# A two-level triangular inverse on TensorE: matrices 0 to 3 and 4 to 7 alternate between two quarters of the array

## The chip, the cores and the metric

The kernel runs on one core of one Trainium2 chip. The metric is the device time of one execution in microseconds (us), the median over runs. The clock that the throttle granted TensorE is listed with each run, as a share of full speed; it was 0.997 in the profiled execution.

## What is computed

The reference is one step of a decoder layer in float32: a gated DeltaNet branch (32 value heads of 128 x 128 state, 16 query and key heads) and a sparse attention branch, on 256 prompt tokens and on 8 samples of 8 tokens, 320 tokens in all; model width 2048. The change touches the delta rule's triangular solve, cut here to what matters (a block has 64 tokens in the reference):

```python
def gated_delta_rule(q, k, v, g, beta, s0):
    # chunked (WY form): S_t = e^{g_t} S_{t-1} + k_t beta_t (v_t - e^{g_t} S_{t-1}^T k_t)^T
    ...
    kb = k * beta[..., None]
    a_strict = jnp.where(strict, jnp.einsum('bhnid,bhnjd->bhnij', kb, k) * decay, 0.0)
    rhs = jnp.concatenate([v * beta[..., None], kb * jnp.exp(G)[..., None]], axis=-1)
    sol = lax.linalg.triangular_solve(a_strict, rhs, left_side=True, lower=True, unit_diagonal=True)
    u_intra, w_state = sol[..., :DV], sol[..., DV:]
    ...
    def chunk_step(s, xs):
        u_c, w_c, qk_c, qd_c, kt_c, gt_c = xs
        u = u_c - jnp.einsum('bhck,bhkv->bhcv', w_c, s)
        o = jnp.einsum('bhck,bhkv->bhcv', qd_c, s) + jnp.einsum('bhij,bhjv->bhiv', qk_c, u)
        s = s * gt_c[..., None, None] + jnp.einsum('bhck,bhcv->bhkv', kt_c, u)
        return s, o
    s, o = lax.scan(chunk_step, s0, xs)
    ...
```

The kernel takes blocks of 128 prompt tokens, and inverts the unit triangular matrices instead of solving with them.

## The kernel before

**The main stream.** `stream()` goes over all weights in half-blocks of 128 x 8 x 128 numbers. For exactness each is split into two parts, `whi` (ScalarE's rounded copy of `raw`) and `wlo` (VectorE's remainder), and so are the activations (`xh`, `xl`). A unit of the stream is 24 matmuls of 128 x 128 x 320 into a main PSUM bank (`pm`): eight pairs `xh,whi` and `xl,whi`, then eight `xh,wlo`. SP loads `raw` several half-blocks ahead (three tiles of two halves).

**The side work.** All else that needs TensorE stands between main matmuls. After the sixth pair of a unit and at its end, so after every 12 main matmuls, `side_round()` steps each of a list of generators once; a step emits its instructions and yields. The program's order is thus fixed when it is built, by a planner (`Clock`) with modelled costs: a generator may yield a due time, and `need(self.ps_side, n)` lets it go on only when n of the side PSUM banks (`ps`, six, 128 x 512 numbers each) are free and, by the model, idle. `psum()` takes the bank that is idle earliest. Each engine runs its own instructions in that order and waits on semaphores where data or buffers come from another. TensorE runs in order, so a side matmul that waits holds the main stream behind it.

**The inverse.** The generator `inverse(g, G)` runs for eight groups g, each of two heads with twelve unit triangular 128 x 128 matrices: eight of the prompt (m = 0 to 7) and four of the samples. The four diagonal 32 x 32 blocks of each matrix go to 48 partitions and are inverted on GpSimd in 31 steps. The result in both orientations goes to DRAM (`d_x[0]`, `d_x[1]`) and comes back spread over partitions, as do the off-diagonal blocks (`d_o`). The tiles: `blk` holds BO (off-diagonal 64 x 64 blocks), BD (off-diagonal 32 x 32 blocks) and Q1; `Xt`, shown as X in the profile, holds XB (inverse, 64-row quarter) and Q2; `XT` is the result, twelve transposed inverses. Then four stages on TensorE build the prompt matrices' off-diagonal parts, each stage one bank and one step of the generator, with at least 12 main matmuls between two stages:

1. Q1 = BD·XB, 32 x 32, in rows 0:32 and 64:96 of the array alternately: 16 matmuls.
2. 32 x 32, the off-diagonal blocks of XT at both 64-row halves, and the lower left block of XB: 24 matmuls.
3. 64 x 64, Q2 = BO·XB, all in rows 0:64 with results in partitions 64:128: eight matmuls.
4. 64 x 64, XT's upper right quarter = −Q2·XT, all in rows 64:128 with results in partitions 0:64: eight matmuls.

ScalarE evicts each result (`self.act`). Behind stage 4 `G["T"] = 4` lets the chains of the group's two heads start (`prompt_chain`, `sample_chain`), which use XT, vt, kq, ktok and w. The tiles of the inverse and XT have one buffer each, so one group's inverse follows the other's.

All loads and stores named here are issued on SP's queue, in program order, among the loads of `raw`.

Of the kernel before, what the change touches and what calls it, by code (L numbers as in the profile page):

```python
# [11 lines left out]
AF = mybir.ActivationFunctionType  # L12
# [189 lines left out]
class Kernel:  # L202
# [1668 lines left out]
    def inverse(self, g, G):  # L1871
        nc = self.nc
        BT = G["BT"]
        d_b, d_x, d_o = self.d_b[g % 2], self.d_x[g % 2], self.d_o[g % 2]
        yield self.ready(BT)
        for k in range(4):
            nc.sync.dma_start(d_b[k].rearrange("m j i -> j m i"), BT[32 * k:32 * k + 32, :, 32 * k:32 * k + 32])
        nc.sync.dma_start(d_o[:, :, 0:64], BT[0:64, 0:8, 64:128])
        for o in (0, 64):
            nc.sync.dma_start(d_o[o // 2:o // 2 + 32, :, 64:96], BT[o:o + 32, 0:8, o + 32:o + 64])  # L1880
        self.BT.put(BT)
        yield
        yield from self.need(self.inv)
        tiles = blk, Xt = self.inv.get()
        yield self.idle(blk, Xt)
        nc.sync.dma_start(blk[0:48], d_b.rearrange("k m j i -> (k m) (j i)"))
        nc.gpsimd.memset(Xt[0:48], 0.0)
        nc.gpsimd.memset(Xt[0:48, 0:1024:33], 1.0)
        yield
        X = Xt[0:48].rearrange("p (i c) -> p i c", c=32)  # L1890
        B = blk[0:48].rearrange("p (j i) -> p j i", i=32)
        for j in range(31):
            n, m = 31 - j, j + 1
            t = self.tmp[:, 0:n * m].rearrange("p (i c) -> p i c", c=m)
            bv = B[:, j, j + 1:32].rearrange("p (i o) -> p i o", o=1).to_broadcast([48, n, m])
            xv = X[:, j:j + 1, 0:m].to_broadcast([48, n, m])
            self.tt(t, bv, xv, OP.mult, eng=nc.gpsimd)
            self.tt(X[:, j + 1:32, 0:m], X[:, j + 1:32, 0:m], t, OP.subtract, eng=nc.gpsimd)
            if j % 4 == 4 - 1:
                yield self.clock.last - 3.6  # L1900
        nc.gpsimd.tensor_copy(blk[0:48].rearrange("p (c i) -> p c i", i=32), X.rearrange("p i c -> p c i"))
        yield
        while not self.XT.free:
            yield
        XT = G["XT"] = self.XT.get()
        XB = Xt[:, 0:512].rearrange("p (m c) -> p m c", c=64)
        Q2 = Xt[:, 512:1024].rearrange("p (m c) -> p m c", c=64)
        BO = blk[:, 0:512].rearrange("p (m c) -> p m c", c=64)
        BD = blk[:, 512:768].rearrange("p (m c) -> p m c", c=32)
        Q1 = blk[:, 768:1024].rearrange("p (m c) -> p m c", c=32)  # L1910
        nc.sync.dma_start(d_x[0].rearrange("k m i c -> (k m) (i c)"), Xt[0:48])
        nc.sync.dma_start(d_x[1].rearrange("k m i c -> (k m) (i c)"), blk[0:48])
        yield max(self.clock.last, self.idle(XT))
        nc.gpsimd.memset(XB[0:32, :, 32:64], 0.0)
        nc.sync.dma_start(BO[0:64], d_o[:, :, 0:64])
        for o in (0, 64):
            nc.sync.dma_start(BD[o:o + 32], d_o[o // 2:o // 2 + 32, :, 64:96])
        for k in range(4):
            s = slice(32 * k, 32 * k + 32)
            nc.sync.dma_start(XT[s, :, s], d_x[1][k].rearrange("m i c -> i m c"))  # L1920
            if k < 3:
                o = 32 * (k % 2)
                nc.sync.dma_start(XB[s, :, o:o + 32], d_x[0][k, 0:8].rearrange("m i c -> i m c"))
        yield
        yield from self.need(self.ps_side)
        p = self.psum()
        pv = p[:, 0:256].rearrange("p (m c) -> p m c", m=8)
        for m in range(8):
            for o in (0, 64):
                self.mm(pv[o + 32:o + 64, m, :], BD[o:o + 32, m, :], XB[o:o + 32, m, 0:32], skip=True)  # L1930
        for o in (32, 96):
            self.act(Q1[o:o + 32], pv[o:o + 32])
        self.ps_side.put(p)
        yield
        yield from self.need(self.ps_side)
        p = self.psum()
        pv = p.rearrange("p (e m c) -> p e m c", e=2, m=8)
        for m in range(8):
            for o in (0, 64):
                self.mm(pv[o:o + 32, 0, m, :], Q1[o + 32:o + 64, m, :], XT[o + 32:o + 64, m, o + 32:o + 64], skip=True)  # L1940
            self.mm(pv[32:64, 1, m, :], XT[32:64, m, 32:64], Q1[32:64, m, :], skip=True)
        for o in (0, 64):
            self.act(XT[o:o + 32, 0:8, o + 32:o + 64], pv[o:o + 32, 0], AF.Copy, scale=-1.0)
        self.act(XB[32:64, :, 0:32], pv[32:64, 1], AF.Copy, scale=-1.0)
        self.ps_side.put(p)
        yield
        yield from self.need(self.ps_side)
        p = self.psum()
        pv = p.rearrange("p (m c) -> p m c", m=8)
        for m in range(8):  # L1950
            self.mm(pv[64:128, m, :], BO[0:64, m, :], XB[0:64, m, 0:64], skip=True)
        self.act(Q2[64:128], pv[64:128])
        self.ps_side.put(p)
        yield
        yield from self.need(self.ps_side)
        p = self.psum()
        pv = p.rearrange("p (m c) -> p m c", m=8)
        for m in range(8):
            self.mm(pv[0:64, m, :], Q2[64:128, m, :], XT[64:128, m, 64:128], skip=True)
        self.act(XT[0:64, 0:8, 64:128], pv[0:64], AF.Copy, scale=-1.0)  # L1960
        self.ps_side.put(p)
        self.inv.put(tiles)
        G["T"] = 4
        self.inverses += 1
# [454 lines left out]
```

## Time and profile before

| | us |
|---|---|
| median of three runs | 2175.32 |
| runs | 2173.44 to 2176.6 |
| profiled execution | 2176.31 |
| its span in the profile | 2174.6 |
| TensorE busy | 2144.6 |
| VectorE busy | 1395.1 |
| ScalarE busy | 995.3 |
| GpSimd busy | 462.2 |

The profiled execution has 1.71 us outside the span. A row of the page's groups gives line, engine, operation, output and inputs by the program's names, the shape and the count, then busy time, the mean in ns and the idle time before. All instructions pass through one helper, so all rows have line L61, and one goes by tile names. An fp32 matmul has two records in the profile: `ps<-XT,X 64*64 64x64 f32 x16` are eight matmuls on a 64 x 64 part of the array with 64 columns each. PE is TensorE's matmuls, PEld its weight loads, DVE VectorE, ACT ScalarE, POOL GpSimd, SPq SP's issue of DMAs. A timeline row begins with its start and duration; consecutive instructions of a group are one row, with their count at the end.

### The profile page before, as it was taken

The page shows a single profiled execution, that of the slowest core. Times are in us where ns is not written, and L with a number is a line of the kernel's source. Part 1 is how long each engine was busy: PE and PEld are TensorE (multiplying, and loading weights), DVE is VectorE, ACT ScalarE, POOL GpSimd, SP SyncE. Part 2 cuts the span into 40 slices and gives each one's busy share as a digit, 9 for nine tenths or more (in the row PEclk, how much of TensorE's full clock was granted, in tenths as well). Part 3 has the DMA queues.
Part 4 walks back from the last instruction along what each step waited for, and adds up shares of the span by engine and source line. Part 5 has one row for each costly group of instructions (what it writes and reads, how often), then busy time and mean ns, then how long its engine had stood idle before and what let it go on. Part 6 is the DMA issues. An engine that isn't in the chain of part 4 may idle for free.

```text
span 2174.6 us, 43708 instructions
## 1 busy us (share of the span) xinstructions
PE 2144.6 (99%) x17071; PEld 2045.5 (94%) x17071; DVE 1395.1 (64%) x2823; ACT 995.3 (46%) x2217; POOL 462.2 (21%) x627
## 2 busy tenths in 40 slices
PE   7999999999999999999999999999999999999997
PEld 6889988999999999899999999999999999999997
DVE  4665545789754577877877777877746545455443
ACT  3225465333343455465555555555545434333343
POOL 1001000000001018353636362626260000000000
PEclk9999999999999999999999999999999999999999
DMA  9995656975688666776768686867786867555562
GB/s 328 356 290 152 172 152 185 273 225 154 180 244 246 192 180 174 203 209 184 206 191 221 176 215 180 217 176 210 185 238 192 261 188 214 166 149 155 156 183 87
DMA packets 715087, 438.38 MB, mean 202 GB/s; under 512 B 69088, under 2 KB 700224, under 8 KB 712576
## 3 DMA queue, kind: packets, MB, share of 16 engines
q1 hardware_dynamic: 710784, 412.92, 67.3%
q0 software_dynamic: 3616, 21.02, 2.9%
q8 instruction: 134, 2.20, 0.4%
q10 hardware_dynamic: 480, 1.65, 0.3%
q14 instruction: 73, 0.60, 0.1%
HBM read 386.29 MB, written 48.94 MB: 200 GB/s over the span
## 4 chain that ended last, share of the span: by engine, by line
PE 68%; issue 23%; DVE 5%; ACT 2%; DMA 2%; SPq 0%; DVEq 0%; POOL 0%; POOLq 0%; ACTq 0%
PE pm L61 52%; PE ps L61 16%; DVE S L61 2%; DMA raw<-in_w_ada_dram 1%; DVE ps L61 1%; ACT ot L61 1%; DVE wlo L61 1%; DVE w L61 0%; ACT whi L61 0%; ACT vt L61 0%; DMA c<-in_c_sample_dram 0%; SPq L61 0%; DVE vt L61 0%; DVE sc L61 0%; DVE sga L61 0%
## 5 line engine op out<-in xcount | busy, mean ns | idle before, releaser
L61 PE MATMUL pm<-xh,whi 128*128 128x320 f32 x3284 | 1004.1, 319 | 2.0 <-ACT whi L61 1.7
L61 PE MATMUL pm<-xl,whi 128*128 128x320 f32 x3284 | 971.6, 309 | 0.3 <-DVE xl L61 0.3
L61 DVE TENSOR_TENSOR wlo<-raw,whi 128x1024 fp32r<-128x1024 f32 x474 | 593.1, 1259 | 291.0 <-ACT whi L61 275.6
L61 PEld LDWEIGHTS pm<-xh,whi 128*128 128x128 f32 x3284 | 616.8, 188 | 39.6 <-issue 31.2
L61 PEld LDWEIGHTS pm<-xl,whi 128*128 128x128 f32 x3284 | 617.5, 188 | 1.6 <-DVE xl L61 0.8
L61 ACT ACTIVATE whi<-raw 128x1024 fp32r<-128x1024 f32 x474 | 498.9, 1059 | 169.1 <-PE pm L61 151.0
L61 PE MATMUL pm<-xh,wlo 128*128 128x320 f32 x3284 | 553.3, 309 | 0.0
L61 PEld LDWEIGHTS pm<-xh,wlo 128*128 128x128 f32 x3284 | 499.5, 188 | 0.0
L61 POOL TENSOR_TENSOR X<-X,tmpx 48x31 f32<-48x31 f32 (+15 forms) x248 | 180.6, 728 | 19.5
L61 POOL TENSOR_TENSOR tmpx<-blk,X 48x31 f32<-48x31 f32 (+15 forms) x248 | 160.4, 647 | 55.1 <-DMA blk<-d_b 23.4
L61 PE MATMUL pm<-y1h,whi 128*128 128x320 f32 x512 | 151.8, 310 | 1.9 <-ACT y1h L61 1.9
L61 PE MATMUL pm<-y1l,whi 128*128 128x320 f32 x512 | 151.9, 310 | 0.1
L61 DVE SCALAR_TENSOR_TENSOR ps<-xp,cs,ps 128x344 f32<-128x344 f32 x192 | 111.5, 581 | 6.8
L61 POOL TENSOR_TENSOR sc<-sc,mh 128x6 f32<-128x6 f32 (+1 forms) x24 | 44.7, 1864 | 324.9 <-DVE ct L61 165.4
L61 POOL TENSOR_TENSOR rfin<-rfin,mh 128x3 f32<-128x3 f32 x1 | 0.8, 848 | 489.4 <-DVE rfin L61 489.4
L61 PEld LDWEIGHTS pm<-y1h,whi 128*128 128x128 f32 x512 | 96.6, 189 | 2.2 <-ACT y1h L61 2.2
L61 PEld LDWEIGHTS pm<-y1l,whi 128*128 128x128 f32 x512 | 96.6, 189 | 0.7 <-DVE y1l L61 0.6
L61 PE MATMUL pm<-y1h,wlo 128*128 128x320 f32 x512 | 86.4, 311 | 0.0
L61 PEld LDWEIGHTS pm<-y1h,wlo 128*128 128x128 f32 x512 | 78.5, 190 | 0.0
L61 DVE SCALAR_TENSOR_TENSOR S<-S,gtr,ps 128x128 f32<-128x128 f32 x256 | 67.4, 341 | 0.1
L61 ACT ACTIVATE ot<-ot,sc 128x128 f32<-128x128 f32 x96 | 29.9, 390 | 74.2 <-DVE sc L61 74.2
L61 ACT ACTIVATE xp<-pm 128x256 f32<-128x256 f32 (+1 forms) x128 | 32.0, 304 | 67.6 <-PE pm L61 67.6
(368 smaller groups left out, 2329.7 us busy)
## 6 DMA issues: line engine op xcount, KB each, us to landing
raw<-in_w_in_dram SPq DMA_DIRECT2D x336, 512.0 KB
raw<-in_w_pa_dram SPq DMA_DIRECT2D x64, 512.0 KB
rawx<-in_w_ada_dram SPq DMA_DIRECT2D x18, 1024.0 KB
a<-in_w_ada_dram SPq DMA_DIRECT2D x16, 1024.0 KB
S<-in_state_gdn_dram SPq DMA_DIRECT2D x32, 512.0 KB
out_dram<-S SPq DMA_DIRECT2D x32, 512.0 KB
raw<-in_w_pb_dram SPq DMA_DIRECT2D x32, 512.0 KB
raw<-in_w_out_dram SPq DMA_DIRECT2D x32, 512.0 KB
```

The costliest lines, as they stand in the source:

```text
L61: made = fn(*args, **kw)
```

## The change

All of it is in `inverse`. Matrices 0 to 3 stay in the quarters of the array where all eight were; matrices 4 to 7 of stages 3 and 4 go to another quarter, and the matmuls alternate between the two. For that BO of matrices 4 to 7 is loaded to partitions 64:128, and a new piece of the tile Xt, XE, holds the inverse's blocks that these matrices need on the other partitions: four more loads from `d_x`, two more memsets on GpSimd. In stage 2, half of the XB products go to the other partitions, and four more products give XE's second block in a second bank; there are three evictions to XB and XE (ahead of XT's two) where there was one. Stage 3 fills one bank's 256 columns on all 128 partitions and has one eviction; stage 4 fills two banks and has two.

```diff
-        Q2 = Xt[:, 512:1024].rearrange("p (m c) -> p m c", c=64)
+        Q2 = Xt[:, 512:768].rearrange("p (m c) -> p m c", c=64)
+        XE = Xt[:, 768:1024].rearrange("p (m c) -> p m c", c=64)
...
         nc.gpsimd.memset(XB[0:32, :, 32:64], 0.0)
-        nc.sync.dma_start(BO[0:64], d_o[:, :, 0:64])
+        nc.gpsimd.memset(XE[32:64, :, 0:32], 0.0)
+        nc.gpsimd.memset(XE[64:96, :, 32:64], 0.0)
+        for e in range(2):
+            nc.sync.dma_start(BO[64 * e:64 * e + 64, 0:4], d_o[:, 4 * e:4 * e + 4, 0:64])
...
+            o, t = 32 * (k % 2), 32 * ((k + 2) % 4)
+            nc.sync.dma_start(XE[t:t + 32, :, o:o + 32], d_x[k // 2][k, 4:8].rearrange("m i c -> i m c"))
...
-        yield from self.need(self.ps_side)
-        p = self.psum()
+        yield from self.need(self.ps_side, 2)
+        p, q = self.psum(), self.psum()
         pv = p.rearrange("p (e m c) -> p e m c", e=2, m=8)
+        qv = q[:, 0:128].rearrange("p (m c) -> p m c", m=4)
         for m in range(8):
             for o in (0, 64):
                 self.mm(pv[o:o + 32, 0, m, :], Q1[o + 32:o + 64, m, :], XT[o + 32:o + 64, m, o + 32:o + 64], skip=True)
-            self.mm(pv[32:64, 1, m, :], XT[32:64, m, 32:64], Q1[32:64, m, :], skip=True)
+            o = 64 * (m // 4)
+            self.mm(pv[o + 32:o + 64, 1, m, :], XT[32:64, m, 32:64], Q1[32:64, m, :], skip=True)
+            if m > 3:
+                self.mm(qv[0:32, m - 4, :], Q1[96:128, m, :], XT[96:128, m, 96:128], skip=True)
+        self.act(XB[32:64, 0:4, 0:32], pv[32:64, 1, 0:4], AF.Copy, scale=-1.0)
+        self.act(XE[96:128, :, 0:32], pv[96:128, 1, 4:8], AF.Copy, scale=-1.0)
+        self.act(XE[0:32, :, 32:64], qv[0:32], AF.Copy, scale=-1.0)
         for o in (0, 64):
             self.act(XT[o:o + 32, 0:8, o + 32:o + 64], pv[o:o + 32, 0], AF.Copy, scale=-1.0)
-        self.act(XB[32:64, :, 0:32], pv[32:64, 1], AF.Copy, scale=-1.0)
...
-        pv = p.rearrange("p (m c) -> p m c", m=8)
-        for m in range(8):
+        pv = p[:, 0:256].rearrange("p (m c) -> p m c", m=4)
+        for m in range(4):
             self.mm(pv[64:128, m, :], BO[0:64, m, :], XB[0:64, m, 0:64], skip=True)
-        self.act(Q2[64:128], pv[64:128])
+            self.mm(pv[0:64, m, :], BO[64:128, m, :], XE[64:128, m, :], skip=True)
+        self.act(Q2, pv)
...
-        yield from self.need(self.ps_side)
-        p = self.psum()
-        pv = p.rearrange("p (m c) -> p m c", m=8)
-        for m in range(8):
-            self.mm(pv[0:64, m, :], Q2[64:128, m, :], XT[64:128, m, 64:128], skip=True)
-        self.act(XT[0:64, 0:8, 64:128], pv[0:64], AF.Copy, scale=-1.0)
+        yield from self.need(self.ps_side, 2)
+        banks = [self.psum() for _ in range(2)]
+        for m in range(4):
+            self.mm(banks[0][0:64, 64 * m:64 * m + 64], Q2[64:128, m, :], XT[64:128, m, 64:128], skip=True)
+            self.mm(banks[1][0:64, 64 * m:64 * m + 64], Q2[0:64, m, :], XE[0:64, m, :], skip=True)
+        for e, p in enumerate(banks):
+            self.act(XT[0:64, 4 * e:4 * e + 4, 64:128], p[0:64, 0:256].rearrange("p (m c) -> p m c", m=4), AF.Copy, scale=-1.0)
```

The planner's model prices the instructions as they are written, so the order moves too. In the first and seventh inverse the stages stand where they stood; in the second and eighth all four stages come one round later; in the third to sixth stages 1 and 2 stand where they stood and stages 3 and 4 come one round later. In those, the first head's chain starts one round later and the second head's catches up with it.

On TensorE in the third inverse, before the change, stage 3 (`ps<-X,blk 64x64`) stands behind half a unit of the main stream after stage 2 (its last row is the first here):

```order
L61 MATMUL ps_72<-blk,XT_7324 32x32
L61 MATMUL pm_66<-xh,whi_78 128x320
L61 MATMUL pm_66<-xl,whi_78 128x320
L61 MATMUL pm_66<-xh,whi_78 128x320
L61 MATMUL pm_66<-xl,whi_78 128x320
L61 MATMUL pm_66<-xh,wlo_81 128x320 x8
L61 MATMUL ps_70<-X,blk 64x64 x8
```

With the change the same stage stands one round later, in the next unit, and stage 4 behind it goes back and forth between two banks and two pairs of inputs (X alone: Q2 and XE):

```order
L61 MATMUL ps_72<-X,blk 64x64 x8
L61 MATMUL pm_66<-xh,whi_79 128x320
L61 MATMUL pm_66<-xl,whi_79 128x320
L61 MATMUL pm_66<-xh,whi_79 128x320
L61 MATMUL pm_66<-xl,whi_79 128x320
L61 MATMUL pm_66<-xh,wlo_82 128x320 x8
L61 MATMUL ps_70<-XT_7324,X 64x64
L61 MATMUL ps_69<-X 64x64
L61 MATMUL ps_70<-XT_7324,X 64x64
L61 MATMUL ps_69<-X 64x64
```

The main stream between stages 3 and 4 is the same 12 matmuls as between 2 and 3 before; only the place of the stages in it has moved.

On SP in the first inverse, before the change, stand one BO load, two BD loads, and then the blocks of XT and XB in turn:

```order
L61 DMA blk<-d_o_96 64x8x64
L61 DMA blk<-d_o_96 32x8x32 x2
L61 DMA XT_7324<-d_x_94 32x12x32
L61 DMA X<-d_x_94 32x8x32
L61 DMA XT_7324<-d_x_94 32x12x32
L61 DMA X<-d_x_94 32x8x32
L61 DMA XT_7324<-d_x_94 32x12x32
L61 DMA X<-d_x_94 32x8x32
```

With the change:

```order
L61 DMA blk<-d_o_96 64x4x64 x2
L61 DMA blk<-d_o_96 32x8x32 x2
L61 DMA XT_7324<-d_x_94 32x12x32
L61 DMA X<-d_x_94 32x8x32
L61 DMA X<-d_x_94 32x4x32
L61 DMA XT_7324<-d_x_94 32x12x32
L61 DMA X<-d_x_94 32x8x32
L61 DMA X<-d_x_94 32x4x32
L61 DMA XT_7324<-d_x_94 32x12x32
L61 DMA X<-d_x_94 32x8x32
```

The third XB load (the last row of each), which stage 1 reads, has one BO and two XE loads more ahead of it on the queue.

On ScalarE in the first inverse, one piece of the difference, from the evictions of stage 1 (`blk<-ps`) to that of stage 3:

```order
 L61 ACTIVATE blk<-ps_71 32x256 x2
 L61 ACTIVATE whi_80<-raw_76 128x1024
+L61 ACTIVATE X<-ps_70 32x4x32 x2
+L61 ACTIVATE X<-ps_67 32x4x32
 L61 ACTIVATE XT_7324<-ps_70 32x8x32 x2
-L61 ACTIVATE X<-ps_70 32x8x32
 L61 ACTIVATE xp_7291<-pm_65 128x256
 L61 ACTIVATE xp_7291<-pm_65 128x8x8
 L61 ACTIVATE xp_7291<-cs_102 128x8x3
-L61 ACTIVATE X<-ps_67 64x512
```

The evictions that stage 3 reads have moved ahead of XT's, and there are two more of them.

More of the change, by code (lines that the diff above doesn't have):

```diff
@@ L1940, in inverse @@
                 self.mm(pv[o:o + 32, 0, m, :], Q1[o + 32:o + 64, m, :], XT[o + 32:o + 64, m, o + 32:o + 64], skip=True)
-            self.mm(pv[32:64, 1, m, :], XT[32:64, m, 32:64], Q1[32:64, m, :], skip=True)
+            o = 64 * (m // 4)
[5 more added lines that the diff above has]
+        self.act(XE[0:32, :, 32:64], qv[0:32], AF.Copy, scale=-1.0)
         for o in (0, 64):
             self.act(XT[o:o + 32, 0:8, o + 32:o + 64], pv[o:o + 32, 0], AF.Copy, scale=-1.0)
-        self.act(XB[32:64, :, 0:32], pv[32:64, 1], AF.Copy, scale=-1.0)
         self.ps_side.put(p)
+        self.ps_side.put(q)
         yield
@@ L1948, in inverse @@
         p = self.psum()
-        pv = p.rearrange("p (m c) -> p m c", m=8)
-        for m in range(8):
+        pv = p[:, 0:256].rearrange("p (m c) -> p m c", m=4)
+        for m in range(4):
             self.mm(pv[64:128, m, :], BO[0:64, m, :], XB[0:64, m, 0:64], skip=True)
-        self.act(Q2[64:128], pv[64:128])
+            self.mm(pv[0:64, m, :], BO[64:128, m, :], XE[64:128, m, :], skip=True)
+        self.act(Q2, pv)
         self.ps_side.put(p)
         yield
-        yield from self.need(self.ps_side)
-        p = self.psum()
-        pv = p.rearrange("p (m c) -> p m c", m=8)
-        for m in range(8):
-            self.mm(pv[0:64, m, :], Q2[64:128, m, :], XT[64:128, m, 64:128], skip=True)
-        self.act(XT[0:64, 0:8, 64:128], pv[0:64], AF.Copy, scale=-1.0)
-        self.ps_side.put(p)
+        yield from self.need(self.ps_side, 2)
[5 more added lines that the diff above has]
+            self.act(XT[0:64, 4 * e:4 * e + 4, 64:128], p[0:64, 0:256].rearrange("p (m c) -> p m c", m=4), AF.Copy, scale=-1.0)
+            self.ps_side.put(p)
         self.inv.put(tiles)
```

## The prediction

> **What bounds the kernel now.** I read the page's busy shares, its clock row and the shares of the chain that ended last, then TensorE's waits, then the windows.
>
> ```profile
> span 2174.6 us, 43708 instructions
> PE 2144.6 (99%) x17071; PEld 2045.5 (94%) x17071; DVE 1395.1 (64%) x2823; ACT 995.3 (46%) x2217; POOL 462.2 (21%) x627
> PEclk9999999999999999999999999999999999999999
> PE 68%; issue 23%; DVE 5%; ACT 2%; DMA 2%; SPq 0%; DVEq 0%; POOL 0%; POOLq 0%; ACTq 0%
> ```
>
> TensorE is busy for 99% of the span at the highest clock digit; the next engine, VectorE, stands at 64%. The chain is TensorE and its own issue for 91%. The waits of TensorE (count, total and so on: the first number is us in all, the second how often) and those of its weight loads say what else there is:
>
> ```profile
> PE pm L61 <- DVE c L61: 7.5, 2, 7.2
> PE pm L61 <- DMA raw<-in_w_ada_dram: 2.8, 2, 1.6
> PE pm L61 <- ACT y1h L61: 1.9, 1, 1.9
> PE pm L61 <- ACT whi L61: 1.7, 6, 0.3
> PE ps L61 <- DVE S L61: 1.1, 2, 0.6
> PEld ps L61 <- DVE w L61: 2.3, 6, 0.4
> ```
>
> No row has to do with the inverse: its four stages are paid as TensorE time, not as waits. One stretch of 109 us in the phase of the eight inverses (columns: window, us, then busy time of PE, PEld, DVE, ACT, POOL, then clock, DMA share, GB/s) shows the same:
>
> ```profile
> 1065.00:1174.00 109.00, 108.58 (x871) 104.04 (x870) 83.50 (x197) 61.50 (x168) 53.00 (x71) 1.00 0.74 200
> ```
>
> TensorE idles 0.42 us of 109. What a stage takes less on TensorE comes off the end time, and work for other engines is free unless TensorE waits for it.
>
> **The stages' price.** From the chain: three stages of the first inverse with a piece of the main stream between them, and the last stage of the seventh inverse (start, us of the slot in the chain, engine, tile, count of records).
>
> ```profile
> 875.67 0.62 PE ps L61 x32
> 878.25 0.63 PE ps L61 x48
> 878.88 1.97 PE pm L61 x12
> 884.33 1.07 PE ps L61 x16
> 1526.07 1.07 PE ps L61 x16
> ```
>
> An fp32 matmul leaves two records, so the 16 matmuls of stage 1 are 32 records, the 24 of stage 2 are 48, the eight of stage 4 are 16. Stages 3 and 4 have the same shape and count:
>
> ```profile
> L61 PE MATMUL ps<-XT,X 64*64 64x64 f32 x128 | 9.1, 221 | 0.0
> L61 PE MATMUL ps<-X,blk 64*64 64x64 f32 x128 | 9.1, 221 | 0.0
> ```
>
> 128 records in eight inverses each, 9.1 us busy in each group, none idle before. In a slot a 64x64 record takes 1.07/16 = 67 ns, one after the other, since before the change all of them use one quarter of the array.
>
> Do matmuls in two parts of the array run beside each other on this chip? Stage 1 alternates rows 0:32 with rows 64:96, stage 2 uses three places. Stage 1 has 32 records of half the columns (32 for 64): one by one they would take about 32 x 33 = 1.06 us, by an estimate from the 67 ns; the slot is 0.62. Stage 2 has half as many records again and takes 0.63. So two and three parts overlap fully, also into one PSUM bank on different partitions, as stage 1 writes. The nearest row for results of two row parts in two banks on the same partitions is in the chains:
>
> ```profile
> 1012.16 0.59 PE L61 MATMUL ps<-w,ktok 128*128 128x256 f32 x2
> 1012.59 0.61 PE L61 MATMUL ps<-vt,PT 128*128 128x128 f32 x4
> 1013.13 1.15 PE L61 MATMUL ps<-w,ktok 32*128 32x256 f32 x16
> 1014.21 0.42 PE L61 MATMUL pm<-xh,whi 128*128 128x320 f32 x1
> ```
>
> Sixteen 32-row records of 256 columns, in four row parts and four banks, start at 1013.13 and the next work starts at 1014.21: 1.08/16 = 67 ns each. The same 256 columns over the full array take 1012.59 − 1012.16 = 0.43 us for two records, 215 ns each. Four parts run at 3.2 times the pace.
>
> **The change part by part.**
>
> *Stage 3.* Eight matmuls, now alternately in rows 0:64 with columns 64:128 and rows 64:128 with columns 0:64, into one bank on different partitions: the pattern of stage 1. Slot from 1.07 to 1.07/2 = 0.535; −0.535 each, −4.3 over eight. Bounds: 0 (no overlap) to −4.3.
>
> *Stage 4.* Eight matmuls alternately in rows 64:128 and 0:64, both to columns 0:64, in two banks: the pattern of the 32-row group. Another −4.3, bounds 0 to −4.3; I take the end, since both near rows overlap in full. Together −8.5.
>
> At one place the Trainium skill speaks against this. Its page "TensorEngine Tiling (Array Packing)", section "Gotcha 1: PSUM Pressure", says that different row tiles cannot access the same PSUM bank simultaneously. By that rule stage 3, which puts two row tiles in one bank, would gain nothing, and the sum would be 4.3 us less. Stage 1 of this trace writes two row tiles into one bank, on different partitions, and takes 0.62 where one after the other would take 1.06: here the trace does not agree.
>
> *Stage 2.* Four matmuls more, in a place that three others share (rows 96:128), and half of the e = 1 products go to another row of columns. Between nothing (stage 2 over stage 1: 16 records more for 0.01 us) and 8 x 0.63/48 = 0.105 us each, 0.84 in all. I take +0.3: for matrices 4 to 7 one part gets two turns, but other parts have slack beside it.
>
> *Pieces on TensorE that only move.* Some stages come a round later (the order shown above), so the main stream is broken at other places. Counted in the order, TensorE passes 722 times from a main bank to a side bank or back, 700 before. In the last view four vt,PT records of 128 columns take 1013.13 − 1012.59 = 0.54, and the two of 256 take 0.43: the 0.11 between them bounds what a border between groups costs. For 22 that is 0 to 2.4 us. I take 0, because that border is also one to small tiles, whose number (113 changes of tile size) stays.
>
> *SP and the loads.* BO comes in two DMAs and XE in four; five more per inverse. An issue of this kind takes SP 0.46 to 0.64 us:
>
> ```profile
> 868.34 1.92 SPq L61 DMA_DIRECT2D blk<-d_o  x3
> 870.30 0.60 SPq L61 DMA_DIRECT2D XT<-d_x  x1
> 872.95 0.47 SPq L61 DMA_DIRECT2D X<-d_x  x1
> 875.60 0.69 PE L61 MATMUL ps<-X,blk 32*32 32x32 f32 x32
> ...
> 1516.70 0.47 SPq L61 DMA_DIRECT2D X<-d_x  x1
> 1518.61 0.69 PE L61 MATMUL ps<-X,blk 32*32 32x32 f32 x32
> ...
> 1620.69 0.47 SPq L61 DMA_DIRECT2D X<-d_x  x1
> 1624.66 0.69 PE L61 MATMUL ps<-X,blk 32*32 32x32 f32 x32
> ...
> 1079.68 0.30 SPq L61 DMA_DIRECT2D X<-d_x  x1
> 1084.56 0.69 PE L61 MATMUL ps<-X,blk 32*32 32x32 f32 x32
> ```
>
> SP is in the chain for 0%, so its 2.6 us more per inverse (0.64 + 4 x 0.47) hurt only where somebody waits for what it issues late. Stage 1 needs the third load of XB, which is each X row here. Ahead of it there are now one BO (1.92/3 = 0.64) and two XE loads (0.94): it is issued 1.58 us later. Before, TensorE began stage 1 2.65 us after that issue in inverse 1, 1.91 in inverse 7, 3.97 in inverse 8. It waited for no DMA in any, so a load lands within 1.91 us. Inverse 8 has 3.97 − 1.58 = 2.39 left: nothing. Inverse 1 has 1.07 left: short by 0 to 0.84. Inverse 7 has 0.33 left: short by 0 to 1.58. The third, in the last two rows, has 4.88, the least of the other five. Sum 0 to 2.4; I take the middle, +1.2, since the landing lies somewhere below 1.91 and nothing shows where. A wait here holds the main stream too, since TensorE goes in order. The raw weights behind these loads on SP are requested several half-blocks ahead; the waits of TensorE above show none for raw in this phase, and 2.6 us is less than two half-blocks (1.97 us for 12 of 24 matmuls). The bytes are small beside 200 GB/s.
>
> *ScalarE.* Five evictions instead of three after stage 2, one half as long after stage 3, two for one after stage 4:
>
> ```profile
> 878.94 0.76 ACT L61 ACTIVATE XT<-ps 32x256 f32<-32x256 f32 x2 [0.69 <-PE ps L61]
> 879.73 0.37 ACT L61 ACTIVATE X<-ps 32x256 f32<-32x256 f32 x1
> 881.96 0.59 ACT L61 ACTIVATE X<-ps 64x512 f32<-64x512 f32 x1 [0.46 <-PE ps L61]
> ```
>
> Two XT of 0.38 and one X of 0.37 become three of half the length, taken at 0.26 each (0.37 less half of the 0.22 between 512 and 256 columns), and two XT: 1.54 for 1.13. Stage 3 needs XB and XE, which now come first: ready 3 x 0.26 = 0.78 us after stage 2 instead of 1.13. That is earlier; XT, ready 0.41 later, is for stage 4 alone, which stands a main piece (1.97) further on. Stage 3's eviction of 128x256 is at 0.38 by this row, for 0.59:
>
> ```profile
> 1103.55 0.38 ACT L61 ACTIVATE w<-ps 128x256 f32<-128x256 f32 x1 [3.21 <-PE ps L61]
> ```
>
> All of it lies beside TensorE; ScalarE is at 61.5 of 109 us there. Cost 0; if the cover goes, the stage 4 pair (2 x 0.37 for 0.59) delays the chains' first use of XT by 0.15 us.
>
> *GpSimd.* Two more memsets, half as wide as this one:
>
> ```profile
> 865.58 0.30 POOL L61 MEMSET X<- 32x256 f32 x1
> ```
>
> At most 0.30 each, ahead of the loads into the same tile's columns; the XE loads come behind the BO and BD issues (1.92 us), which covers them. Cost 0.
>
> *Order.* In inverses 2 and 8 all stages, in 3 to 6 the last two, come one round (12 main matmuls, about 2 us) later, and the first head's chain starts later by that; the second head's catches up. Only TensorE's waits on others can change by this: the row for w, 2.3 us in six places, is the part that lies in the chains. I take 0, and ±1.7 as bounds.
>
> Sum: −8.5 + 0.3 + 1.2 = −7.0. The profiled execution took 2176.31 us (1.71 outside the span) and would take 2169.3. It stands 1.0 above the median of the runs, 2175.32; against that the forecast is 2168.3. The size of the gain, 0.32%, is above what a measurement of this kernel tells from no change, about 0.2% (4.35 us).
>
> The likeliest case's own range: best −8.5 − 1.7 = −10.2, 2165.1; worst −8.5 + 0.84 + 2.4 + 2.4 + 1.7 = −1.2, 2174.1, if every bound is met at once.
>
> **The rivals.**
>
> *A: one of the two stages does not overlap.* For stage 4 what could fail is that two row parts send sums down the same columns 0:64; for stage 3, that both write one bank. The 32-row group speaks against the first, stage 1 against the second; but neither has 64-row parts. Gain −7.0 + 4.3 = −2.7: 2172.6, no measurable change. Chance 0.11: 0.06 for stage 4, 0.05 for stage 3. The second is also what the quoted rule of the Trainium skill would give.
>
> *B: the later order gives the gain back.* Chains that start a round later and catch up stand closer together, so that TensorE meets sums which ScalarE or VectorE has not evicted yet. For it: an eviction in a chain waits for TensorE and then takes about 0.4 us, and the weight-load wait for w has 0.4 us at a time now, six times. Against: the planner still puts other work between. One us in each of the six moved inverses is 6: −7.0 + 6 = −1.0, 2174.3, no measurable change. Chance 0.14.
>
> *C: slower, by late loads.* If a 32-partition load landed only some 1.9 us after its issue, and SP were slower with these issues than in the first inverse, stage 1 would wait in all inverses. For it: the same three issues took longer in the second inverse,
>
> ```profile
> 959.11 3.21 SPq L61 DMA_DIRECT2D blk<-d_o  x3
> ```
>
> 3.21 for 1.92, so 1.07 each. It decides from a wait of 8.5/8 = 1.06 us per inverse; with 1.6 us (the whole shift of the loads) it is −8.5 + 0.3 + 12.8 = +4.6, 2179.9. Against: six inverses have 3.97 us of room or more. Chance 0.08.
>
> **How the numbers follow.** The main case has 0.67, A 0.11, B 0.14, C 0.08. The predicted time is the main case's, 2168.3. Faster by over 0.2% means below 2170.97; the main case has some of its worst ends above that, and about as much chance of A and B lies below: faster 0.67, same 0.25, slower 0.08. For the range I leave out C and the outermost of the main case and of B, which is about 2 in 10: from 2164.5 (the best end less 0.6 for the runs' spread, 2173.44 to 2176.6) to 2174.1, the worst end, which takes in A and part of B.
>
> **What would show it.** In the profile after, stages 3 and 4 stand in the chain or the timeline with about 0.54 us from start to next start, not 1.07 (the sum of the stages). Stage 2 stands at 0.63 to 0.74 with 56 records. The weight-load or matmul waits of TensorE have a row for X <- d_x of at most 2.4 us in all, in inverses 1 and 7; a larger row is C. The wait for w stays near 2.3; if it and those for ps rise by several us, it is B. If stage 3 or 4 keeps 1.07, it is A. ScalarE and GpSimd stay out of the list of TensorE's waits for this work.

## The result, and the profile after

| | us, median | runs |
|---|---|---|
| before | 2174.38 | 2172.72 to 2176.6 (6) |
| after | 2162.82 | 2160.82 to 2165.01 (6) |
| ratio | 0.9949 | 95% interval 0.9939 to 0.9960 |

The change makes the kernel 11.6 us faster by the medians, 0.5%. A second set of runs on another occasion gave 2161.48 against 2172.9, the same ratio, 0.9949 (0.9936 to 0.9963). The prediction was 7.0 us faster than the first three runs of before (2175.32), so 2168.3, with a range from 2164.5 to 2174.1. The sign is right, and the time lies below the range.

The page of the changed kernel, the rows that answer to those of before:

```profile
span 2160.4 us, 43967 instructions
PE 2132.3 (99%) x17135; PEld 2036.1 (94%) x17135; DVE 1392.0 (64%) x2823; ACT 997.6 (46%) x2241; POOL 464.0 (21%) x643
PEclk9999999999999999999999999999999999999999
PE 70%; issue 23%; POOL 2%; DMA 2%; DVE 1%; SPq 1%; ACT 0%; DVEq 0%; POOLq 0%; ACTq 0%
```

TensorE bounds the kernel as before; POOL's 2% in the chain is the way back from the one wait for a load of the inverse to GpSimd's steps ahead of it. TensorE's waits, matmuls first, then the rows of the weight loads (us in all, times, longest):

```profile
PE pm L61 <- DVE c L61: 7.6, 2, 7.3
PE ps L61 <- DMA X<-d_x: 1.2, 1, 1.2
PE pm L61 <- ACT y1h L61: 1.0, 1, 1.0
PE pm L61 <- ACT whi L61: 0.3, 1, 0.3
PEld ps L61 <- DVE w L61: 0.4, 1, 0.4
```

Two rows differ that the prediction did not expect to: `whi` was 1.7 in 6 waits and is 0.3 in one, `w` was 2.3 in 6 and is 0.4 in one. One row is new, X <- d_x, as expected. The chain shows where that is, and the stages' slots:

```profile
873.25 2.67 DMA X<-d_x
875.96 0.69 PE ps L61 x30
878.60 0.66 PE ps L61 x50
884.22 0.61 PE ps L61 x16
```

This is inverse 1. The third XB load is issued at 873.25 and released TensorE 2.67 us later. Stage 2 takes 0.66 us where 0.63 stood. The last row is a 64-row stage: 0.61 us where 1.07 stood.

Because the main stream is the same in all kernels, the distance between stage 1 of the third and of the sixth inverse is a clock for three groups. Before, the sixth begins at

```profile
1412.03 0.69 PE L61 MATMUL ps<-X,blk 32*32 32x32 f32 x32
```

and the distance is 1412.03 − 1084.56 = 327.47 us; a second profile of before has exactly that again (1411.60 − 1084.13). After:

```profile
1082.20 0.69 PE L61 MATMUL ps<-X,blk 32*32 32x32 f32 x32
...
1404.16 0.69 PE L61 MATMUL ps<-X,blk 32*32 32x32 f32 x32
```

321.96, so 5.51 less for three groups, 1.84 for one. The stages explain 2 x (1.07 − 0.61) = 0.92 of that. Stage 2 takes 0.03 of it back. The other half, some 0.93 per group, belongs to the term that the prediction put at 0, the order.

### The profile page after: what moved, and what is told of

The parts are those of the page before. It is cut to its first block, busy times and chain, and to the rows that moved or that the text cites. A ratio compares the mean times of both kernels' runs of the same rounds, so it can differ in the third digit from the quotient of the medians.

```text
span 2160.4 us, 43967 instructions
## 1 busy us (share of the span) xinstructions
PE 2132.3 (99%) x17135; PEld 2036.1 (94%) x17135; DVE 1392.0 (64%) x2823; ACT 997.6 (46%) x2241; POOL 464.0 (21%) x643
## 4 chain that ended last, share of the span: by engine, by line
PE 70%; issue 23%; POOL 2%; DMA 2%; DVE 1%; SPq 1%; ACT 0%; DVEq 0%; POOLq 0%; ACTq 0%
PE pm L61 53%; PE ps L61 17%; DMA raw<-in_w_ada_dram 1%; POOL X L61 1%; POOL tmpx L61 1%; SPq L61 1%; DVE S L61 1%; DMA c<-in_c_sample_dram 0%; DMA blk<-d_b 0%; DMA out_dram<-S 0%; DMA raw<-in_w_in_dram 0%; ACT ot L61 0%; DVE wlo L61 0%; DMA X<-d_x 0%; DVE sga L61 0%
```

## The experiments

Theory 1 was that the other half comes from the order: in the second to sixth group the stages, and with them the chains, stand a round later, and the waits for `w` and `whi` go. Theory 2 was that these waits go because the stages are shorter and are evicted sooner. In the pinned kernels a step of the inverse waits for a given round instead of for the planner; three lines more at the top make the helper's line L64. The kernels below that keep the order of the change are pinned to it as well. Each kernel is compared with runs of before on the same chip; their medians are 2173.41, 2173.07 and 2172.9.

**Order alone (first try).**

```diff
+PINS = [[309, 352, 399, ...], ...]   # round of each stage, by inverse: those of the change
...
-        yield from self.need(self.ps_side)
+        while self.rnd < PINS[0][self.inverses] or len(self.ps_side.free) < 1:
+            yield 0.0
```

> The kernel before, its arithmetic, loads and evictions untouched; only the rounds in which the four stages of the inverse stand are pinned to those of the change, and all side work on TensorE then stands in the order of the change. Theory 1 (the order gives what the overlap does not explain): the wait of main matmuls for whi falls from 6 times to 1 and that of w,ktok for w from 6 to 1, 0.9 us in each of five groups, 4.5 us in all; the wait for y1h at the end of the phase falls too, 1.0 to 2.5 us. Time 2174.4 - 4.5 = 2169.9, down to 2167.4 with y1h. Theory 2 (these waits went because the new stages are shorter and evicted sooner): no row changes, 2174.4.

2170.24 against 2173.41, ratio 0.9985 (0.9976 to 0.9994): near the time of theory 1, but only because before is lower here than the 2174.4 of the expectation: the gain is 3.2 us, not 4.5. The three-group distance is 1409.15 − 1082.93 = 326.22, 0.42 per group less. In the window of the third group the wait for `w` is gone and that for `whi` is in two halves (last row):

```profile
1082.93 0.69 PE L64 MATMUL ps<-X,blk 32*32 32x32 f32 x32
...
1409.15 0.69 PE L64 MATMUL ps<-X,blk 32*32 32x32 f32 x32
...
PEld pm L64 <- ACT whi L64: 0.4, 2, 0.2
```

TensorE stood in the order of the change, GpSimd did not. Its steps for the next group ran beside VectorE's part of the norm. VectorE's and GpSimd's timeline there:

```profile
1118.71 0.76 DVE L64 TENSOR_TENSOR sc<-sc,sc 128x6 f32<-128x6 f32 x2
...
1117.78 1.47 POOL L64 TENSOR_TENSOR X<-X,tmpx 48x192 f32<-48x192 f32 x1
```

**Order alone, GpSimd too.** The kernel before, every step of the inverse pinned, those on GpSimd and the loads too. One of the places:

```diff
-            if j % 4 == 4 - 1:
-                yield self.clock.last - 3.6
+            if j % 4 == 4 - 1:
+                while self.rnd < PINS[g][at]:
+                    yield 0.0
+                at += 1
```

> The kernel before with its arithmetic, loads and evictions; all steps of the inverse are pinned to the rounds of the change, also those on GpSimd and its loads, which the first order experiment left free (there GpSimd began the next group's 31 steps ahead of the norm's sc, and that came late). Theory 1 (order alone takes both waits away): per group 0.9 us, whi and w once each, 5 x 0.9 = 4.5 us under before in the profile, and about 1 us of y1h: 2173.4 - 5.5 = 2167.9. Theory 2 (the wait for whi needs the shorter stages as well): 0.4 per group as in the first order experiment, 2170.2.

2168.03 against 2173.07, ratio 0.9976 (0.9967 to 0.9985). 5.0 us come with no change in arithmetic.

```profile
1082.62 0.69 PE L64 MATMUL ps<-X,blk 32*32 32x32 f32 x32
...
1407.29 0.69 PE L64 MATMUL ps<-X,blk 32*32 32x32 f32 x32
...
PE pm L64 <- ACT whi L64: 0.3, 1, 0.3
PEld ps L64 <- DVE w L64: 0.4, 1, 0.4
```

324.67: 2.80 less for three groups, 0.93 per group, and both waits are at one, as in the changed kernel. Theory 1 holds for the whole other half; theory 2 falls. The two VectorE operations on 128x6 that took 0.76 beside GpSimd took 0.35 here, with GpSimd idle:

```profile
1118.21 0.35 DVE L64 TENSOR_TENSOR sc<-sc,sc 128x6 f32<-128x6 f32 x2
...
1118.85 1.32 POOL L64 TENSOR_TENSOR sc<-sc,mh 128x6 f32<-128x6 f32 x1 [26.81 <-DVE sc L64]
```

That GpSimd's activity is what kept 0.5 us per group in the first try is read from these rows; this kernel moved GpSimd's steps and the loads together, and neither was switched by itself.

**The new arithmetic in the old order.** The changed kernel, its stages pinned to the rounds of before.

> The changed kernel with its stages pinned to the rounds of the kernel before, so that TensorE has the order of before. Theory 1: only the overlap is left, 8 x 0.92 = 7.4 us, less 1.2 for the late load in inverse 1: 2174.4 - 6.2 = 2168.2; the waits for whi and w stand at 6 times each, as before. Theory 2: the waits are gone as in the changed kernel, 2162.8.

2169.5 (2166.75 to 2172.12) against 2173.41, ratio 0.9983 (0.9974 to 0.9992). Its profile is of the fastest run, with

```profile
1081.76 0.69 PE L64 MATMUL ps<-X,blk 32*32 32x32 f32 x32
...
1406.58 0.69 PE L64 MATMUL ps<-X,blk 32*32 32x32 f32 x32
...
PE pm L64 <- ACT whi L64: 1.7, 6, 0.3
PEld ps L64 <- DVE w L64: 2.3, 6, 0.4
PEld ps L64 <- DMA X<-d_x: 1.2, 1, 1.2
```

324.82, 0.88 per group less, the share of the stages alone (0.92 less 0.03 for stage 2); both waits stand six times as before. So the two halves add up: 0.93 + 0.88 = 1.81 for 1.84. The wide spread pointed to the late loads (the row for X is now in inverse 7). The next kernel tests that.

**The same, XE loads last.**

```diff
             if k < 3:
                 o = 32 * (k % 2)
                 nc.sync.dma_start(XB[s, :, o:o + 32], d_x[0][k, 0:8].rearrange("m i c -> i m c"))
+        for k in range(4):
             o, t = 32 * (k % 2), 32 * ((k + 2) % 4)
             nc.sync.dma_start(XE[t:t + 32, :, o:o + 32], d_x[k // 2][k, 4:8].rearrange("m i c -> i m c"))
```

> The changed arithmetic in the order of before (as in the second experiment), with the four XE loads issued behind those of XT and XB. Theory 1 (that experiment's runs were spread from 2166.8 to 2172.1 because stage 1 waited for the XB load behind XE, more or less by the run): no wait for X, 0.9 us per inverse, 7.3 in all, and about 1 us of y1h: 2165.1, and a spread like that of the other kernels, 2 to 3 us. Rival (the spread is from something else in that order): median and spread stay, 2169.5.

2166.61 (2165.88 to 2167.66) against 2173.07, ratio 0.9970 (0.9958 to 0.9982): 2.9 us below the median of the one before and a spread of 1.8 for 5.4. By these runs, 11 of the one and six of the other, the place of the XE loads is what spread it. It did not remove the wait altogether: one of 0.6 us for X <- d_x is left in inverse 7.

**XE loads last, in the order of the change.** The same edit.

> The changed kernel in its own order on TensorE, with the four XE loads issued behind all loads of XT and XB. Theory 1 (the 1.2 us wait of inverse 1 for X <- d_x is the two XE loads ahead of the third XB load): the row is gone, 2162.8 - 1.2 = 2161.6. Rival (the loads land late because of what else is in the queues, not because of their place): the row stays at 1 us or more, 2162.8.

2160.91 against 2173.41, ratio 0.9945 (0.9931 to 0.9958). The row for X <- d_x is gone, but one profile does not show that the edit took it away: the second profile of the change has no such row either (below). The runs say more. They are 12.5 us under before, where the change is 11.4 to 11.6 under it, and they spread over 1.3 us (2160.38 to 2161.64), where those of the change spread over 4.2 and 3.3.

**Grouped instead of alternating.**

```diff
         for m in range(4):
             self.mm(pv[64:128, m, :], BO[0:64, m, :], XB[0:64, m, 0:64], skip=True)
+        for m in range(4):
             self.mm(pv[0:64, m, :], BO[64:128, m, :], XE[64:128, m, :], skip=True)
```

and the same in stage 4.

> The changed kernel in its own order, but in stages 3 and 4 the four matmuls of matrices 0 to 3 come first and then the four of 4 to 7, instead of alternating. Theory 1 (two quarters run beside each other only where neighbours in the order use different ones): the two stages stand at about 1.0 us again, 0.058 us x 7 x 16 = 6.5 us more, 2169.3. Rival (the gain is from shorter runs per bank or from the evictions, or TensorE overlaps the groups anyway): 2162.8.

2166.05 against 2173.41, ratio 0.9970 (0.9958 to 0.9982): 7.4 us under before, where the change is 11.4 to 11.6 under it. So the loss is about 4, not the 6.5 of theory 1 nor the 0 of the rival. The slots of stages 3 and 4 say why, and so do the records of stage 4 (`ps<-XT,X` is the first group, `ps<-X` the second):

```profile
1089.84 0.89 PE ps L64 x16
1092.68 0.89 PE ps L64 x16
```

```profile
1092.61 0.50 PE L64 MATMUL ps<-XT,X 64*64 64x64 f32 x5
1092.90 0.27 PE L64 MATMUL ps<-X 64*64 64x64 f32 x1
1092.95 0.22 PE L64 MATMUL ps<-XT,X 64*64 64x64 f32 x1
...
1093.12 0.45 PE L64 MATMUL ps<-X 64*64 64x64 f32 x5
```

0.89 lies between 0.61 and 1.07. The first record of the second group starts at 1092.90, ahead of the last three of the first group, though it stands behind them in the program. So three of the eight records of each group run in pairs, and five of each run alone. The alternation is worth 2 x 0.28 us per inverse, 4.5 us in all.

**Another round later in the seventh group (a miss, then mended).** Of the six waits each for `w` and `whi` one is left, in the seventh group, whose stages 3 and 4 the change did not move.

> The changed kernel with the XE loads behind the others, and stages 3 and 4 of the seventh inverse one round later, as the change has them in the third to sixth. Theory 1 (the later round takes the waits for w and whi away): the last two of these waits go, 0.9 us: 2160.9 - 0.9 = 2160.0. Rival (the seventh group differs): 2160.9 or more.

2163.62 against 2173.07, ratio 0.9955 (0.9941 to 0.9969): 9.5 us under before, worse than the 12.5 without the edit. This kernel also issued BO behind the other loads, which is not in its expectation, and so the planner's chains of the second to sixth group moved too: 1406.59 − 1082.93 = 323.66 for the three groups instead of 321.96. The second group alone, from its stage 1 to that of the third, takes 107.79 us instead of 106.01.

```profile
1082.93 0.69 PE L64 MATMUL ps<-X,blk 32*32 32x32 f32 x32
...
1406.59 0.69 PE L64 MATMUL ps<-X,blk 32*32 32x32 f32 x32
```

With BO back in its place, this is the kernel of "XE loads last, in the order of the change" with one edit, stages 3 and 4 of the seventh inverse one round later:

```diff
-PINS = [..., [311, 354, 402, 450, 498, 546, 593, 641], [312, 355, 403, 451, 499, 547, 594, 642]]
+PINS = [..., [311, 354, 402, 450, 498, 546, 594, 641], [312, 355, 403, 451, 499, 547, 595, 642]]
```

> The kernel of the fourth experiment (XE loads last, BO where the change has it) with stages 3 and 4 of the seventh inverse one round later. The run before this one also issued BO behind the other loads, and the planner then moved the chains of groups 2 to 6 as well, which cost 0.5 to 1.1 us per group in its profile. Theory: groups 2 to 6 are as in the changed kernel (1.8 us per group under before), the seventh gives 1.9 instead of 1.0, the waits for w are gone and that for whi in the phase too: 0.9 under the fourth experiment, 2160.0. Rival (what slowed groups 2 to 6 there is the later seventh round): 2163 again.

2160.18 (2158.86 to 2160.31) against 2172.9, ratio 0.9937 (0.9923 to 0.9950), and 1.3 us under the changed kernel on the same chip. The waits of matmuls in the whole phase are down to two rows:

```profile
PE ps L64 <- DVE S L64: 1.1, 2, 0.6
PE pm L64 <- ACT y1h L64: 1.1, 1, 1.1
```

No wait for `whi` is left. This version beats both kernels: all its runs lie below those of the change. How much of that the seventh group gives, the medians do not tell: it is 12.7 us under its own before, and the kernel without this edit was 12.5 under its own, 0.2 less, not 0.9. The profiles do: from stage 1 of the seventh inverse to that of the eighth they have 1613.64 − 1507.70 = 105.94 us with the edit and 1615.00 − 1508.10 = 106.90 without it, 0.96 less.

**The change and before once more.**

> The kernel before, profiled a second time. If its wait of 2.2 us for y1h at 1706 us and the reduced clock behind it belong to that kernel, they are here too. If they are chance (all four experiments and the change have 0 to 1.4 us there), they are smaller here, about 1 us, with no reduced clock, and the profiled execution of before stood 2 to 3 us too high against the others. All else, the six waits for whi and for w, stays.

> The changed kernel once more, on the same chip as the one above, with a second profile. Theory: 11.2 us under before (stages 7.3, order 4.5, y1h and startup chance, less 1.4 for the late load of inverse 1), the wait for X <- d_x in inverse 1 between 0.5 and 1.5 us again, one wait each for w and whi left. Rival (the 1.2 us of the load was chance): no row for X <- d_x, and 2161.

Before: 2173.2, and the six waits each for `whi` and `w` again. But the wait of the main matmuls for y1h, an input of theirs that ScalarE makes at the end of the phase, is shorter: 1.1 us for 1.9. In the first profile of before the wait is followed by a stretch at a lower granted clock. The first row below is the first profile, from the end of the wait on, the second the same place in the second one (window, us, busy times, then clock, DMA share, GB/s):

```profile
1709.00:1714.00 5.00, 4.89 (x21) 4.66 (x22) 4.54 (x6) 3.55 (x5) 0.00 (x0) 0.66 0.80 244
```

```profile
1707.40:1712.40 5.00, 4.87 (x31) 4.65 (x32) 4.54 (x6) 4.13 (x6) 0.00 (x0) 1.00 0.80 246
PE pm L61 <- ACT y1h L61: 1.1, 1, 1.1
```

The first profiled execution of before thus stood 2.7 us too high there (from a main matmul ahead of that place to one behind it, against the second profile). The spans of the two first profiles, 14.2 us apart, overstate the change by that; the medians do not.

After: 2161.48, and no row for X <- d_x, so the wait that was expected again did not come. The third XB load stands in the row `X<-d_x x2` below (it is the first of the two), and stage 1 begins 3.07 us later:

```profile
872.49 0.96 SPq L61 DMA_DIRECT2D X<-d_x  x2
...
875.56 0.69 PE L61 MATMUL ps<-X,blk 32*32 32x32 f32 x32
```

In the first profile the stage began only 1.3 us after that issue (874.55 against 873.25). TensorE's and SP's positions against each other differ by the execution by more than 1 us, and so the wait is there in one profile of two. The grouped kernel, with the same loads in the same order, had it too: stage 1 began 1.39 us after that issue (874.22 against 872.83) and waited 1.0 us.

## Why the prediction was wrong, and where it was right

| term | predicted | measured | by |
|---|---|---|---|
| stages 3 and 4 | −8.5 | −7.4 (8 x 0.92) | slots 1.07 to 0.61 |
| stage 2 | +0.3 | +0.2 (8 x 0.03) | slot 0.63 to 0.66 |
| load waits | +1.2 | +1.2 in one profile, 0 in the other | row for X <- d_x |
| breaks, ScalarE, GpSimd | 0 | no row | waits |
| order | 0 ± 1.7 | −4.6 (5 x 0.93) | order alone |

The measured terms give −11.8 without the load wait and −10.6 with it; the medians say −11.6 and −11.4.

**The step that failed is the order.** The prediction said that "only TensorE's waits on others can change by this", and that is right. It then counted only the row for `w` with 2.3 us, took zero for the term and ±1.7 as its bounds. The kernel with the order alone showed −4.6. Three things were wrong. The row `whi`, 1.7 us in six waits, stood in the quoted list and was left out. Both rows count six: once in each group from the second to the seventh, so they are tied to a place in the chain and go or stay together, five times 0.93 (0.4 for `w`, the rest for `whi` and its weight load; the seventh group, which kept its place, kept both). And a bound of both signs around zero says that nothing is known, though the profile shows on what the two waits hang. The chain that ended last in the third group of before, VectorE and ScalarE ahead of the main matmul that waits:

```profile
1127.66 1.89 DVE S L61 x7
1129.56 1.14 DVE wlo L61
1130.69 0.44 DVE sc L61
1131.15 1.87 ACT ot L61 x6
1133.02 1.08 ACT vt L61 x3
1134.10 0.96 ACT whi L61
1135.10 0.99 PE pm L61 x5
```

VectorE is late with the updates of S and the norm's sc, ScalarE therefore with `ot` and `vt`, and the copy `whi`, which is queued behind them, reaches TensorE late. In the changed order the same piece is ready ahead of its use:

```profile
1126.77 1.87 ACT L61 ACTIVATE ot<-ot,sc 128x128 f32<-128x128 f32 x6 [5.39 <-DVE sc L61]
...
1129.62 1.05 ACT L61 ACTIVATE whi<-raw 128x1024 fp32r<-128x1024 f32 x1
...
1130.98 0.31 PE L61 MATMUL pm<-xh,whi 128*128 128x320 f32 x1
```

`whi` ends at 1130.67 and is used at 1130.98; before, the copy for the same matmul ended at 1135.06 and TensorE had waited for it. That the order takes both waits away is shown by the kernel with the order alone. Why it does is read from these rows and not shown by a run of its own: a round more between the inverse and its chains, with the same work, gives VectorE time to finish the norm's sc earlier against TensorE. The first try fits this, since there sc was late beside GpSimd and half of the gain was missing. Rival B looked at the right mechanism and had the wrong sign.

**The size of stages 3 and 4** was taken as 1.07/2. A slot is not all pitch (the time from one record's start to the next). From the starts of the records in the trace the pitch within the group is 58 ns, not 67; what is left of 1.07, 1.07 − 16 x 0.058 = 0.14 us, is paid where the small tiles begin and end, and does not halve: 0.14 + 8 x 0.058 = 0.60, measured 0.61. The same sum gives the grouped kernel, with 13 starts in place of 16: 0.14 + 13 x 0.058 = 0.89. The part that does not halve is 1.1 of the 8.5 us.

**Right:** that the two quarters overlap, in both stages. The Trainium skill's rule that was weighed (page "TensorEngine Tiling (Array Packing)", section "Gotcha 1: PSUM Pressure") would have left stage 3, with two row tiles in one bank, at 1.07. Stage 3 and stage 4 both take 0.61 here, so the trace does not agree with the rule for results on different partitions of a bank. Rival A is out. Right too: stage 2 nearly free, ScalarE and GpSimd hidden, the load wait in inverse 1. That a load lands within 1.91 us was wrong as a bound for every inverse: the chain shows 2.67 in inverse 1. Inverse 7, where up to 1.6 us were expected, did not wait: in the changed order its loads are issued one raw load earlier, and the third XB load, the first of the two here, is 3.88 us ahead of stage 1.

```profile
1505.07 1.08 SPq L61 DMA_DIRECT2D X<-d_x  x2
...
1508.95 0.69 PE L61 MATMUL ps<-X,blk 32*32 32x32 f32 x32
```

Rival C did not come. Two numbers of the prediction are off without bearing on the sum: SP's five issues are 2.5 us by the prediction's own terms, not 2.6, and by the records' starts TensorE changes the tile size 347 times in both traces, not 113; that this number stays is right.

## What to carry to other kernels

When an edit moves work in a saturated engine's order, list every wait of that engine which recurs once per iteration and follow each back to what it hangs on: they are the part that a new order can give or take, and here that was 40% of the gain. A slot's price had a part here that did not scale (0.14 of 1.07 us), so take the pitch from the starts within a group, not from slot over count. And profile the kernel before twice when the last 0.1% matters: one profile here held 2.7 us of chance.

## What the runs showed of the hardware

- The 64x64 fp32 matmuls in two quarters of the array ran beside each other at 58 ns a pair of records, in one bank (on different partitions) as in two: 0.61 us for 1.07. They did so as neighbours in the order; four and four in a row overlapped only in part (0.89 us).
- In the grouped kernel a record for the free quarter started at 1092.90, ahead of three that stand before it in the program and use the busy quarter (the first of them at 1092.95).
- After a wait of 1.9 us for y1h, the granted clock was 0.66 over the next 5 us in one profile of before; after a wait of 1.1 us it stayed at 1.00 in the other. The Trainium skill, page "TensorE: Matmul & The Clock Gate", section "Part 1: The HAM clock gate", puts the drop behind an idle window of about 3.4 us; this trace does not agree: it shows the drop after a wait of 1.9 us, once.
- Two VectorE operations on 128x6 took 0.76 us while GpSimd computed (order alone, first try), and 0.35 while it was idle (order alone, GpSimd too).
